# Further row tiles in seven products: third strips of the feed-forward parts, z's first and v's second block, the attention output's first block

## The chip, the cores and the metric

The kernel runs on one core of one Trainium2 chip. What counts is the device time of one execution, in microseconds. The time before is the median of three runs, 2545.25 us (2544.47 to 2546.2).

## What is computed

A trunk of two layers over x of 256 rows (T) and 2048 columns (D), all in float32, with weights that are read once per execution. The parts that matter here, of the reference:

```python
def swiglu(x, w_gate, w_up, w_down):
    return (jax.nn.silu(x @ w_gate) * (x @ w_up)) @ w_down

# layer 0: norm, one input projection, two mixers, one output projection
proj = (xn @ w_in).astype(f32)                    # q, k, v, o, gates, z, x, B, C, dt
...
y = y.reshape(b, s, SSD_D_INNER) * jax.nn.silu(z)
...
mixed = jnp.concatenate([hm, y], axis=-1).astype(xn.dtype)
return mixed @ w_out

# layer 1: norm, attention with 16 heads of 128
qkv = (xn @ w_qkv).astype(jnp.float32).reshape(b, s, 3, ATTN_HEADS, ATTN_HEAD_DIM)
...
o = o.transpose(0, 2, 1, 3).reshape(b, s, D_MODEL).astype(xn.dtype)
return o @ w_o
```

Each layer ends with x + swiglu(norm(x)), with 5632 hidden columns.

## The kernel before

**A product.** To keep float32 accuracy, each factor is split into a high and a low part in a shorter type, and each product is three matmuls: high by high, high by low, low by high. A weight tile `raw` (two row tiles of 128 by two strips of 512 columns, 512 KB) comes by a DMA that SyncE issues. ScalarE casts its high part, `wh` (L450); VectorE subtracts it and leaves the low part, `wl` (L452). `raw`, `wh` and `wl` live in buffers that rotate over three (`raw` has a fourth), so the cast for a tile waits until TensorE has done with the third tile before it.

**A block** (`block`) is one product of x with two strips of 512 columns: eight steps (six in a down projection with three strips), one for each pair of row tiles of the weights. A plan, a string of letters, gives the kind of each step; `pairs` says which row tile pairs the steps S take, in this order, and the steps P take the rest in ascending order.
- P, a plain step: 24 matmuls of 512 columns into four accumulators `acc_f` (F), which fill two double banks, `both`. Two casts, and two subtractions of 128x1024.
- S, a step in seven products (the scheme of Strassen and Winograd on two by two blocks: row tiles by columns): 21 matmuls, into F and into four more accumulators `acc_e` (E1, E7, E5, E6 in banks 4, 5, 6, 7). VectorE makes four sums of weights (L459 two of them, L460, L462), and then there are high and low parts of `raw` (three of its four pieces) and of `sums`. The factors on the other side are sums of x's blocks: `sums_of` and `activation_sums` (L331, L315 to L318), split again into high (ScalarE) and low (VectorE, L225), kept in a tile `skx` or `skh`.

After the last S of a block, E1 is copied to `pre` (L530), and E6, E7, E5 are added to it; after the last step F's accumulators are added (L1036 for z, L1067 in the feed-forward part, L961 in an output projection), which frees the banks.

**Order.** Each engine runs its instructions in a fixed order, which a scheduler makes from priorities: `high_priority` puts the parts of weights 800 places ahead, what empties `pre` 1600. Some pieces are put off (`later`, `transpose_later`) and run between steps: above all the transposes of y and of h, whose results `p_tr` sit in the same banks 6 and 7 as E5 and E6. Between the first and the last S of a block, none of them runs (`held`). Where a piece is needed sooner, `need` runs it.

**Places.** z is 2048 columns of the input projection in two blocks, q = 0 with `PLAN_LATE`, q = 1 with `PLAN_X`. While z's first block runs, the mLSTM output is turned (tiles `mx`, L226 on ScalarE, L227 on VectorE). The feed-forward part (`ffn`) takes the hidden columns in groups of 4, 4 and 3 strips of 512; each strip i is one block, `hidden`, of gate and up columns together, and after each group `add_blocks` multiplies the group's h with its rows of the down weights, in two blocks. The second strip (i = 1) of each group has `PLAN_X4` with four S steps, and makes the sums of pair 7 ahead of its fourth step; the other strips have `PLAN_X` with three. h's first block is summed as soon as it is turned, for the down projection (`skh`). v is made in two blocks (q = 0 `PLAN_LATE`, q = 1 `PLAN_X`). The attention output is added in two blocks, the first with `PLAN_O`, while the last heads (`attend_turn`: `p_pt`, copied to `pT`; `attend_out`: `p_o`, split into `o`) are still on their way.

## Time and profile before

| | |
|---|---|
| median of three runs | 2545.25 us (2544.47 to 2546.2) |
| the profiled execution | 2544.58 us |
| its span in the trace | 2542.8 us |
| granted TensorE clock | 0.999 |
| ScalarE, casts of weights and of their sums (L450) | 623.0 and 256.6 us busy |
| VectorE, low parts of weights and of their sums (L452) | 740.8 and 298.5 us busy |
| VectorE, sums of weights (L459, L460, L462) | 152.4, 85.7 and 85.7 us busy, 125 steps |

In the profile's rows PE is TensorE (matmuls), PEld its weight loads, DVE VectorE, ACT ScalarE, POOL GpSimd, SP SyncE. A row of a timeline has the start in us, the length, the engine, the line of the kernel, the operation, what it writes and reads, the shape, and how many in a row; in brackets the idle time ahead of it and what ended that. A row of the windows has, after the stretch, its length and for each engine the busy time with the number of instructions; then the granted clock, the share of DMA and GB/s. Lengths of one engine's instructions overlap a little in these rows, so that the price of one is the distance to the start of the next.

### The profile page before, as it was taken

To read this page: it belongs to the slowest core of one execution; us is meant where nothing else is said; L and a number is where in the kernel's file an instruction comes from. 1 tells how busy PE (TensorE), PEld (TensorE's weight loads), DVE (VectorE), ACT (ScalarE), POOL (GpSimd) and SP (SyncE) were. 2 spreads that over 40 slices of the span, in tenths; PEclk is the share of its full clock that TensorE was granted. 3 is DMA by queue.
4 is the path that set the end of the run, shared out by engine and by line. 5 is a ranking of instruction groups with operands and counts; after the bars stand their busy time and mean duration, and the time that the engine had idled before them with its cause. 6 is when DMAs were issued, how large, how long until landed. Compare 5 with 4: busy or idle time off the path is not lost.

```text
span 2542.8 us, 32518 instructions
## 1 busy us (share of the span) xinstructions
PE 2529.4 (99%) x12099; PEld 2118.3 (83%) x12099; DVE 2227.9 (88%) x2839; ACT 1483.9 (58%) x1968; POOL 48.5 (2%) x97
## 2 busy tenths in 40 slices
PE   9999999999999999999999999999999999999998
PEld 8888888888888888888888888888888888888887
DVE  5775788898989999999999986767999999999998
ACT  6465565566656655555455665666565555555564
POOL 1000000000000000000000000000000000000000
PEclk9999999999999999999999999999999999999999
DMA  8565575565565657565666656554556566656664
GB/s 289 174 214 180 170 227 171 177 209 188 191 218 178 224 175 231 192 222 187 218 206 208 198 175 231 165 167 146 199 191 208 200 204 215 214 198 197 227 200 166
DMA packets 256383, 505.40 MB, mean 199 GB/s; under 512 B 15976, under 2 KB 16128, under 8 KB 255712
## 3 DMA queue, kind: packets, MB, share of 16 engines
q1 hardware_dynamic: 249952, 483.20, 58.4%
q0 software_dynamic: 4976, 17.43, 1.8%
q10 hardware_dynamic: 1296, 2.69, 0.3%
q8 instruction: 95, 1.56, 0.2%
q14 instruction: 64, 0.52, 0.1%
HBM read 492.66 MB, written 2.14 MB: 195 GB/s over the span
## 4 chain that ended last, share of the span: by engine, by line
PE 95%; DVE 2%; DMA 1%; issue 1%; ACT 0%; POOL 0%; SPq 0%; POOLq 0%; DVEq 0%; ACTq 0%
PE acc_f L484 18%; PE acc_f L486 18%; PE acc_f L485 18%; PE acc_w L393 11%; PE acc_w L397 6%; PE acc_e L484 4%; PE acc_e L485 4%; PE acc_e L486 4%; PE acc_a L424 2%; PE acc_a L423 2%; PE acc_a L422 2%; PE p_tr L284 1%; DMA raw<-in_l_w_o 1%; PE p_y L919 1%; DVE wl L452 0%
## 5 line engine op out<-in xcount | busy, mean ns | idle before, releaser
L450 ACT CAST wh<-raw 128x1024 fp32r<-128x1024 f32 (+1 forms) x563 | 623.0, 1147 | 387.0 <-PE acc_f L486 313.8
L452 DVE TENSOR_TENSOR wl<-raw,wh 128x1024 fp32r<-128x1024 f32 (+1 forms) x563 | 740.8, 1338 | 84.8 <-ACT wh L450 81.4
L484 PE MATMUL acc_f<-wh,x 128*128 128x512 f32 x1086 | 424.8, 391 | 0.0
L486 PE MATMUL acc_f<-wh,x 128*128 128x512 f32 x1086 | 423.0, 389 | 0.0
L485 PE MATMUL acc_f<-wl,x 128*128 128x512 f32 x1086 | 422.7, 389 | 0.0
L450 ACT CAST wh<-sums 128x1024 fp32r<-128x1024 f32 x250 | 256.6, 1051 | 277.6 <-PE acc_f L486 135.0
L379 DVE TENSOR_TENSOR wl<-raw,wh 128x1024 fp32r<-128x1024 f32 x223 | 269.9, 1222 | 115.7 <-ACT wh L378 113.8
L378 ACT CAST wh<-raw 128x1024 fp32r<-128x1024 f32 x223 | 230.7, 1048 | 183.9 <-PE acc_w L393 94.7
L452 DVE TENSOR_TENSOR wl<-sums,wh 128x1024 fp32r<-128x1024 f32 x250 | 298.5, 1219 | 12.3 <-ACT wh L450 11.8
L393 PE MATMUL acc_w<-xa,wh 128*128 128x512 f32 x768 | 264.6, 395 | 1.2 <-DVE xa L227 1.2
L484 PEld LDWEIGHTS acc_f<-wh,x 128*128 128x128 f32 x1086 | 203.9, 188 | 43.0 <-DVE pre L1067 1.4
L486 PEld LDWEIGHTS acc_f<-wh,x 128*128 128x128 f32 x1086 | 203.9, 188 | 42.6
L485 PEld LDWEIGHTS acc_f<-wl,x 128*128 128x128 f32 x1086 | 203.9, 188 | 41.8
L397 PE MATMUL acc_w<-xa,wl 128*128 128x256 f32 x768 | 208.1, 281 | 0.5 <-DVE wl L379 0.5
L393 PE MATMUL acc_w<-x,wh 128*128 128x512 f32 x512 | 182.2, 399 | 0.0
L393 PEld LDWEIGHTS acc_w<-xa,wh 128*128 128x128 f32 x768 | 143.8, 188 | 31.7 <-ACT wh L371 1.5
L459 DVE TENSOR_TENSOR sums<-raw 128x1024 f32<-128x1024 f32 x125 | 152.4, 1219 | 7.0 <-DMA raw<-in_l_w_out 1.9
L397 PEld LDWEIGHTS acc_w<-xa,wl 128*128 128x128 f32 x768 | 142.0, 189 | 2.1 <-DVE wl L379 0.8
L397 PE MATMUL acc_w<-x,wl 128*128 128x256 f32 x512 | 143.3, 280 | 0.0
L393 PEld LDWEIGHTS acc_w<-x,wh 128*128 128x128 f32 x512 | 96.2, 188 | 20.5 <-DVE rsrc L430 0.4
L484 PE MATMUL acc_e<-wh,skx 128*128 128x512 f32 x261 | 101.7, 391 | 0.0
L486 PE MATMUL acc_e<-wh,skx 128*128 128x512 f32 x261 | 101.6, 389 | 0.0
(364 smaller groups left out, 4678.6 us busy)
## 6 DMA issues: line engine op xcount, KB each, us to landing
raw<-in_l_w_in SPq DMA_DIRECT2D x191, 512.0 KB, 3.8
raw<-in_l_ffn_gate SPq DMA_DIRECT2D x176, 512.0 KB, 4.0
raw<-in_l_ffn_up SPq DMA_DIRECT2D x176, 512.0 KB, 4.9
raw<-in_l_ffn_down SPq DMA_DIRECT2D x176, 512.0 KB, 5.1
raw<-in_l_w_qkv SPq DMA_DIRECT2D x96, 512.0 KB, 4.6
raw<-in_l_w_out SPq DMA_DIRECT2D x64, 512.0 KB, 4.9
raw<-in_l_w_o SPq DMA_DIRECT2D x32, 512.0 KB, 4.7
hr<-h POOLq DMA_DIRECT2D x32, 256.0 KB, 3.2
```

Source lines behind the costliest of these rows:

```text
L378: nc.scalar.copy(wh[:, ks, :], raw[:, ks, :])
L379: turn["low"] = nc.vector.tensor_sub(wl[:, ks, :], raw[:, ks, :], wh[:, ks, :].bitcast(F32))
L393: return nc.tensor.matmul(banks[f], wh[:, kk, f * P:(f + 1) * P], kt.both(k0 + kk), start=k0 + kk == 0, stop=False, skip_group_check=True)
L397: nc.tensor.matmul(banks[f][:, :T], wl[:, kk, f * P:(f + 1) * P], kt.parts(k0 + kk)[0], start=False, stop=k0 + kk == nk - 1, skip_group_ch ...
L422: nc.tensor.matmul(banks[t], xh[:, ts], wh[:, kk, :], start=k0 + kk == 0, stop=False)
L423: nc.tensor.matmul(banks[t], xh[:, ts], wl[:, kk, :], start=False, stop=False)
L450: nc.scalar.copy(h[:, c, :], of[:, c, :])
L452: nc.vector.tensor_sub(l[:, c, :], of[:, c, :], h[:, c, :].bitcast(F32))
L459: nc.vector.tensor_sub(sums[:, 0:2, :], raw[:, 2:4, :], raw[:, 3:0:-2, :])
L484: nc.tensor.matmul(dst, ah, bh, start=start, stop=False)
L485: nc.tensor.matmul(dst, ah, bl, start=False, stop=False)
L486: nc.tensor.matmul(dst, al, bh, start=False, stop=stop)
```

## The change

Nine plain steps become steps in seven products:
- z's first block: the plan "PPPSPSPP" becomes `PLAN_Z`, "PPPSPSSP", with the pairs 3, 5, 1 instead of 3 and 5: the new S comes right behind the second one, with the pair 1, whose sums were made in this block already for the one that follows; the plain steps are those of 0, 2, 4, 6, 7.
- the third strip (i = 2) of each of the six groups: `PLAN_X4` instead of `PLAN_X`. The sums of pair 7 are made in the second strip alone and used in the third too.
- v's second block: `PLAN_X4` instead of `PLAN_X`, with the sums of pair 7 made here.
- the attention output's first block: "PPPPPSPP" becomes "PPPPPSSP", with S for the pairs 1 and 3. The plain step of pair 6 then comes as the fifth, before both, and so do all heads of the last group.

```diff
--- before.py
+++ after.py
@@ -38,7 +38,8 @@
 PLAN_X = "PSPSPSPP"
 PLAN_X4 = "PSPSSPSP"
 PLAN_LATE = "PPPSPSPP"
-PLAN_O = "PPPPPSPP"
+PLAN_Z = "PPPSPSSP"
+PLAN_O = "PPPPPSSP"
 PLAN_SEAM = "PPPPSPSP"
 PLAN_H = {4: ("PSPSPSPP", "PSPSPSPP"), 3: ("PSPSPP", "PSPSPP")}
 PLAN_H_LATE = "PPSPSP"
@@ -1026,8 +1027,8 @@
             nc.scalar.activation(halves[i], halves[i], AF.Copy, scale=rr[:, i:i + 1])
 
     for q in range(2):
-        F, pre, _, _ = block(tuple((w_in, C_Z + (2 * q + n) * STRIP) for n in range(2)), xt0, 0, KD, PLAN_X if q else PLAN_LATE,
-                       ahead=((5, scale_gated, 0),) if q else ((4, sums_of, xt0, 1),))
+        F, pre, _, _ = block(tuple((w_in, C_Z + (2 * q + n) * STRIP) for n in range(2)), xt0, 0, KD, PLAN_X if q else PLAN_Z,
+                       pairs=(1, 3, 5) if q else (3, 5, 1), ahead=((5, scale_gated, 0),) if q else ((4, sums_of, xt0, 1),))
         if q == 0:
             for s in range(4):
                 need(("y", s))
@@ -1060,7 +1061,7 @@
         def hidden(hT, i, s, plan, copied):
             more = plan == PLAN_X4
             _, pre, both, joined = block(((wg_, s * STRIP), (wu_, s * STRIP)), xt, 0, KD, plan, pairs=(1, 3, 5, 7) if more else None,
-                                         ahead=((3, sums_of, xt, 7, False),) if more else ())
+                                         ahead=((3, sums_of, xt, 7, False),) if more and i == 1 else ())
             hs = []
             for t in range(NT):
                 with tc.high_priority(offset=1600):
@@ -1081,7 +1082,7 @@
             hT = KT(f"h{name}{first}", 4 * n)
             hT.sums = summed(PLAN_H[n][0])
             for i in range(n):
-                hidden(hT, i, first + i, PLAN_X4 if i == 1 else PLAN_X if first + i else PLAN_LATE, i < n - 1)
+                hidden(hT, i, first + i, PLAN_X4 if i in (1, 2) else PLAN_X if first + i else PLAN_LATE, i < n - 1)
             last = first + n == DFF // STRIP
             add_blocks(wd, hT, first * STRIP, 4 * n, (PLAN_H[n][0], PLAN_H_LATE if last and whole is None else PLAN_H[n][1]),
                        *((finish, begin, whole) if last else ()), pairs=list(hT.sums))
@@ -1169,7 +1170,8 @@
 
     vv = []
     for q in range(2):
-        F, pre, _, _ = block(tuple((w_qkv, 2 * D + (2 * q + n) * STRIP) for n in range(2)), xt2, 0, KD, PLAN_X if q else PLAN_LATE)
+        F, pre, _, _ = block(tuple((w_qkv, 2 * D + (2 * q + n) * STRIP) for n in range(2)), xt2, 0, KD, PLAN_X4 if q else PLAN_LATE,
+                             pairs=(1, 3, 5, 7) if q else None, ahead=((3, sums_of, xt2, 7),) if q else ())
         need("rope")
         for i in range(4):
             with tc.high_priority(offset=1600):
```

The scheduler places the instructions anew. No load is added, taken away or put in another place in SyncE's queue, nor is anything on GpSimd's. TensorE has 27 matmuls fewer, VectorE 42 instructions more, ScalarE 10. Line numbers of the changed kernel are one higher than those of before (two from v's block on), as the rows below show.

In z's first block, VectorE before, where the bank of the turned tile `p_tr_5069` is emptied (`mx3`), and the sums 5176 are those of the second S step:

```order
L227 SCALAR_TENSOR_TENSOR mx3_4897<-p_tr_5027,pv_129,mx3_4897 128x256
L462 TENSOR_TENSOR sums_5176<-raw_5173,sums_5176 128x512
L227 SCALAR_TENSOR_TENSOR mx3_4897<-p_tr_5069,pv_129,mx3_4897 128x256 x2
L452 TENSOR_TENSOR wl_5224<-raw_5220,wh_5223 128x1024
L452 TENSOR_TENSOR wl_5185<-sums_5176,wh_5184 128x1024 x2
L452 TENSOR_TENSOR wl_5224<-raw_5220,wh_5223 128x1024
```

And in the changed kernel, where 5214 are the sums of the third S step:

```order
L463 TENSOR_TENSOR sums_5176<-raw_5173,sums_5176 128x512
L461 TENSOR_TENSOR sums_5214<-raw_5211,sums_5214 128x512
L228 SCALAR_TENSOR_TENSOR mx3_4897<-p_tr_5027,pv_129,mx3_4897 128x256
L463 TENSOR_TENSOR sums_5214<-raw_5211,sums_5214 128x512
L453 TENSOR_TENSOR wl_5218<-raw_5211,wh_5217 128x1536
L228 SCALAR_TENSOR_TENSOR mx3_4897<-p_tr_5069,pv_129,mx3_4897 128x256
L453 TENSOR_TENSOR wl_5223<-sums_5214,wh_5222 128x1024 x2
L228 SCALAR_TENSOR_TENSOR mx3_4897<-p_tr_5069,pv_129,mx3_4897 128x256
L460 TENSOR_TENSOR sums_5345<-raw_5342 128x1024
L453 TENSOR_TENSOR wl_5185<-sums_5176,wh_5184 128x1024 x2
```

The second of the two `mx3` instructions on `p_tr_5069` now stands behind the low parts of the new step, `wl_5218` and `wl_5223`, and those of the second step, `wl_5185`, come after it.

ScalarE at the same place in the changed kernel, where `wh_5217` and `wh_5222` are the new step's high parts, and `pre_5249` the block's first result:

```order
L227 ACTIVATE mx3_4897<-p_tr_5069,pv_129 128x256
L451 CAST wh_5179<-raw_5173 128x1536
L451 CAST wh_5217<-raw_5211 128x1536
L451 CAST wh_5222<-sums_5214 128x1024 x2
L227 ACTIVATE mx3_4897<-p_tr_5069,pv_129 128x256
L531 COPY pre_5249<-acc_e_5111 128x512
L451 CAST wh_5184<-sums_5176 128x1024 x2
```

The last piece of `mx3` stands behind the casts of the new step; before it stood right behind `wh_5179`.

The second place is the end of the third strip in the group of three of the first feed-forward part, VectorE. Before, in the last S step of this strip (sums 11746), with `skh_11547`, the sums of h's first block:

```order
L452 TENSOR_TENSOR wl_11755<-sums_11746,wh_11754 128x1024
L462 TENSOR_TENSOR sums_11746<-raw_11743,sums_11746 128x512
L1071 SCALAR_TENSOR_TENSOR h_11557<-pre_11487,r1_7062,h_11557 128x512
L225 TENSOR_TENSOR skh_11547<-sf_11542,skh_11547 128x4x128
L452 TENSOR_TENSOR wl_11755<-sums_11746,wh_11754 128x1024
```

And in the changed kernel, where the sums 11958 and 12033 belong to the first and the second S step of the down projection that follows, and `skh_11562` are the sums of h's first block:

```order
L453 TENSOR_TENSOR wl_11967<-sums_11958,wh_11966 128x1024
L460 TENSOR_TENSOR sums_12033<-raw_12030 128x1024
L453 TENSOR_TENSOR wl_11967<-sums_11958,wh_11966 128x1024
L453 TENSOR_TENSOR wl_12001<-raw_11997,wh_12000 128x1024 x2
L461 TENSOR_TENSOR sums_12033<-raw_12030,sums_12033 128x512
L226 TENSOR_TENSOR skh_11562<-sf_11557,skh_11562 128x4x128
L463 TENSOR_TENSOR sums_12033<-raw_12030,sums_12033 128x512
```

`skh` was made inside the strip, and is now made behind the low parts of the down projection's first S step (`wl_11967`) and of the plain step after it (`wl_12001`).

## The prediction, made before the result was known

> **What bounds the kernel.** I read the page first: its shares of busy time, then the chain that ended last.

> ```profile
> span 2542.8 us, 32518 instructions
> PE 2529.4 (99%) x12099; PEld 2118.3 (83%) x12099; DVE 2227.9 (88%) x2839; ACT 1483.9 (58%) x1968; POOL 48.5 (2%) x97
> PE 95%; DVE 2%; DMA 1%; issue 1%; ACT 0%; POOL 0%; SPq 0%; POOLq 0%; DVEq 0%; ACTq 0%
> ```

> TensorE is on 95% of the chain: a matmul taken out is worth its time, unless the one behind it then waits. VectorE, at 88%, is what it would wait for. Next I read the timeline of PE for the price of a matmul.

> ```profile
> 1239.84 0.39 PE L484 MATMUL acc_f<-wh,ha 128*128 128x512 f32 x1
> ...
> 1241.65 0.39 PE L486 MATMUL acc_f<-wh,ha 128*128 128x512 f32 x1
> ```

> These are the first and the last of nine matmuls, eight starts apart: 1.81/8 = 0.227 us each. The 0.39 us is a length that overlaps the next one's; the pitch is what counts.

> Then the price of a step on VectorE, from its timeline in the third strip of a three-strip group. Starts are again what counts.

> ```profile
> 1368.13 2.35 DVE L452 TENSOR_TENSOR wl<-raw,wh 128x1024 fp32r<-128x1024 f32 x2
> 1370.40 1.22 DVE L459 TENSOR_TENSOR sums<-raw 128x1024 f32<-128x1024 f32 x1
> 1371.53 1.75 DVE L452 TENSOR_TENSOR wl<-raw,wh 128x1536 fp32r<-128x1536 f32 x1
> 1373.20 0.69 DVE L460 TENSOR_TENSOR sums<-raw,sums 128x512 f32<-128x512 f32 x1
> 1373.80 1.22 DVE L452 TENSOR_TENSOR wl<-sums,wh 128x1024 fp32r<-128x1024 f32 x1
> 1374.94 0.69 DVE L462 TENSOR_TENSOR sums<-raw,sums 128x512 f32<-128x512 f32 x1
> 1376.21 0.69 DVE L225 TENSOR_TENSOR skh<-sf,skh 128x512 fp32r<-128x512 f32 x1
> ```

> A plain step costs 2.27 us there (1368.13 to 1370.40). A step of seven products costs 1.13 + 1.67 + 0.60 + 1.14 + 0.60 and one more 1.14 (the second sums piece): 6.28 us, so 4.0 us more. Last, how much room VectorE has, by stretches: here the six blocks of a four-strip group, of which the first stretch is about a third strip, then the third strip of a three-strip group, and v's second block.

> ```profile
> 840.00:882.00 42.00, 42.00 (x190) 34.55 (x190) 41.55 (x46) 25.11 (x27) 1.08 (x2) 1.00 0.65 216
> 882.00:924.00 42.00, 42.00 (x191) 34.82 (x191) 38.96 (x43) 24.29 (x26) 1.08 (x2) 1.00 0.64 214
> ...
> sum 255.00, PE 255.00 PEld 210.64 DVE 239.89 ACT 142.76 POOL 3.23; mean PE 42.50 PEld 35.11 DVE 39.98 ACT 23.79 POOL 0.54
> 1351.00:1392.30 41.30, 41.30 (x187) 34.12 (x187) 40.84 (x44) 25.25 (x29) 1.07 (x2) 1.00 0.69 229
> 1490.00:1531.50 41.50, 41.50 (x186) 34.35 (x186) 36.38 (x40) 23.57 (x26) 0.00 (x0) 1.00 0.59 195
> ```

> The third column of busy time is VectorE's. Over a whole group 255.0 − 239.9 = 15 us are free, but in a third strip only 0.45 us of 42 (0.46 of 41.3 in the group of three), and 3.0 in the fourth strip (the second row). v's second block has 5.1 us free.

> **The change, part by part.**

> *The gain.* Nine steps go from 24 to 21 matmuls: 27 × 0.227 = 6.1 us, 0.68 us each. This much is sure as far as PE's instruction count goes; all else is what PE then waits for. [...]

> *z's first block (one step): +3.2 us net.* Two steps of seven products now stand side by side, and a PSUM bank that a transposed tile (p_tr_5069) still holds is freed too late. Rows of before, VectorE, ScalarE and PE:

> ```profile
> 527.53 0.48 DVE L227 SCALAR_TENSOR_TENSOR mx<-p_tr,pv,mx 128x256 fp32r<-128x256 f32 x1
> 528.55 0.48 DVE L227 SCALAR_TENSOR_TENSOR mx<-p_tr,pv,mx 128x256 fp32r<-128x256 f32 x1 [0.55 <-ACT mx L226]
> 530.82 1.23 DVE L452 TENSOR_TENSOR wl<-raw,wh 128x1024 fp32r<-128x1024 f32 x1 [1.79 <-ACT wh L450]
> 528.04 0.48 ACT L226 ACTIVATE mx<-p_tr,pv 128x256 fp32r<-128x256 f32 x1 [4.17 <-DVE mx L227]
> 530.70 1.99 ACT L450 CAST wh<-sums 128x1024 fp32r<-128x1024 f32 x2
> 531.99 0.39 PE L486 MATMUL acc_e<-wh,xa 128*128 128x512 f32 x1
> ```

> In before both mx pieces on VectorE are done at 529.0, two of them in a row, with 1.79 us idle after them. In the changed order the second one stands behind wl_5223 x2, the low parts of the new step's sums, and ScalarE's piece behind the casts wh_5222 x2. Those casts need a buffer of the three that rotate: wh_5143's went to wh_5217, so it is wh_5179's, whose last reader is the PE row above, at 531.99; three matmuls of the bank (acc_e_5123) now come behind it, so 531.99 − 0.68 = 531.31, ended at 531.7. Two casts take 1.99: 533.7. VectorE's second subtraction follows, 1.2: 534.9, then mx, 0.48: the bank is free at about 535.5. PE gets to acc_e_5123 ten matmuls after 531.31, at 533.6, and 0.3 later for wl_5218, made just too late: 533.9. **It waits 1.6.** Only then are the last readers of wh_5099 done (three matmuls, 0.7: 536.2), whose buffer wh_5184's casts need: 1.0 for the first, 1.0 for the second, and wl_5185 1.2 behind. PE has four matmuls ready, and waits 1.3 + 0.5. With 0.2 for the later start of z's second block: 0.3 + 1.6 + 1.8 + 0.2 = 3.9, less 0.68: 3.2. Bounds: −0.7 (all hidden, if the casts find a buffer earlier) and +4.5 (0.6 more at the seam to the second block, the size of a 512-wide piece). I take 3.2, nearest to the rows.

> *Third strips of four-strip groups (four steps): −0.1 each.* Nothing in before shows a third strip with four such steps, but its second strips already have four, and two more sums of x. There PE is late only where the next strip begins. Rows of before at such a seam:

> ```profile
> 846.42 1.05 ACT L450 CAST wh<-sums 128x1024 fp32r<-128x1024 f32 x1 [4.00 <-PE acc_f L486]
> 846.81 0.46 PE L484 MATMUL acc_e<-wh,x 128*128 128x512 f32 x1
> 847.18 0.50 PE L484 MATMUL acc_f<-wh,x 128*128 128x512 f32 x1
> ```

> The cast waits for the buffer of the last plain step; PE starts 0.37 apart where 0.23 is usual (0.14), and some 0.1 more at the next. The changed third strip gets this seam too: 0.25. VectorE enters the next strip 4.0 later, with 3 us free there, and pre's evacuation (L1067) holds a bank that the strip's second half needs: about 0.3 more, a bound from the 0.68 of one such 512 piece. 0.6 − 0.68 = −0.1 each, −0.4 in all. The four sums of pair 7 that are not made again cost nothing: they are kept from the second strip. Ends: −0.4 each (seam alone) and +2 (below).

> *Third strips of three-strip groups (two): +1.8 each.* After them comes the down projection, whose second step needs the sums of the first h block (skh). In before it was ready at 1376.21, inside the strip. Now the low part's instruction stands behind the first step's wl, the next plain step's wl x2 and a sum. Rows of before:

> ```profile
> 1394.57 2.35 DVE L452 TENSOR_TENSOR wl<-sums,wh 128x1024 fp32r<-128x1024 f32 x2
> 1396.84 1.22 DVE L459 TENSOR_TENSOR sums<-raw 128x1024 f32<-128x1024 f32 x1
> 1399.35 0.39 PE L484 MATMUL acc_f<-wh,skh 128*128 128x512 f32 x1
> ```

> VectorE is done with those wl at 1396.84 in before; now + 4.0 for the new step, + 1.13 (L459 of the next one, moved ahead), − 1.2 (skh and one ha piece, moved behind), − 0.46 (what was idle): 1400.3. Then wl x2 2.27, a sum 0.60, skh 0.69: **1403.9**. PE's first matmul with skh was at 1399.35; now 0.68 earlier, two matmuls moved ahead (0.45) and 0.3 at the seam: 1399.4. That one and the second read only the high part, which ScalarE makes; the one that reads the low part comes ten later: 1401.7. It waits 2.2, from which I take 0.2 for idle that I count double. With the seam's 0.3 and 0.2 for the bank behind it: 2.5 − 0.68 = 1.8. Twice: +3.6. Ends: −0.4 (VectorE 2 us earlier than I add up) and +3 each.

> *v's second block (one): −0.7.* VectorE idles in the block, waiting for ScalarE (the first three rows); the last two are pieces of a sum of x, as another block makes it:

> ```profile
> 1510.73 2.36 DVE L452 TENSOR_TENSOR wl<-raw,wh 128x1024 fp32r<-128x1024 f32 x2 [1.97 <-ACT wh L450]
> 1519.36 1.23 DVE L452 TENSOR_TENSOR wl<-sums,wh 128x1024 fp32r<-128x1024 f32 x1 [1.12 <-ACT wh L450]
> 1531.14 3.71 DVE L452 TENSOR_TENSOR wl<-raw,wh 128x1024 fp32r<-128x1024 f32 x3 [0.98 <-ACT wh L450]
> ...
> 1766.59 0.67 DVE L331 TENSOR_TENSOR xg<-o 128x512 f32<-128x512 f32 x1
> 1767.30 0.29 DVE L315 TENSOR_TENSOR sf<-xg 128x128 f32<-128x128 f32 x1
> ```

> These, and the 5.1 us of the stretch, take the 4.0 of the step; the extra sums of x (two pieces of 512, 0.6 from start to start, and four of 128, 0.2 each: 2.0) take the rest, 6.0 against 5.1 and the lead that VectorE has. Ends −0.7 and +0.6, if the rest falls on the seam.

> *Attention output's first block (one): +0.5.* The plain step of pair 6 goes two steps ahead, and with it the last two heads' p_o, whose pT copies stand behind the new order's two sums casts:

> ```profile
> 1769.01 1.99 ACT L450 CAST wh<-sums 128x1024 fp32r<-128x1024 f32 x2 [0.41 <-PE acc_f L486]
> 1771.43 0.85 ACT L1159 COPY pT<-p_pt 128x384 f32<-128x384 f32 x2
> 1770.56 0.38 PE L1166 MATMUL p_o<-pT,v 128*128 128x128 f32 x2
> ```

> In before PE had another plain step between the p_o of heads 0 and 1 (done at 1770.9) and those of 2 and 3. Now the latter follow at once. Casts done at 1770.9, the copies 0.4 each: 1771.3 and 1771.7; PE, ready at 1770.9, waits 0.4 for the first, and up to 0.4 more for the second and the casts of o. 0.7, and 0.5 for a later evacuation at the second block's start, less 0.68: +0.5. Ends −0.7 and +1.5. SP's queue gets no other order of loads and no more of them, and POOL's stays as it is: nothing there.

> *The sum.* 3.2 − 0.4 + 3.6 − 0.7 + 0.5 = +6.2. The profiled execution took 2544.58 us (span 2542.8), 0.67 under the median of 2545.25. 2544.58 + 6.2 = 2550.8; set against the median, 2551.4. I predict 2551.

> **Rivals.** The bound for a difference is 0.2%, 5.1 us either way.

> A. *VectorE's lead hides it all*: −6.1, 2538.4 to 2539. For it: 15 us free in each group, 1.79 idle in z just where the new sums stand. It needs the low part of skh by 1401.7 (2.2 us sooner than I add up) and z's bank by 533.6 (1.9 sooner): both orders speak against it. [...] In v's block the rows bear it out, at the seams they don't.

> B. *One of the two large stalls isn't there*: without z's 3.9, +2.3 (2546.9); without the two 2.2 at the down projection, +1.8 (2546.4). Both large stalls rest on a chain of four or five steps with some 0.3 us error each, and one earlier release is enough. Within 0.2%.

> C. *VectorE's deficit stays inside the third strips*: 40.85 or so busy and 4.0 more against 40.6 us of PE: 4 us late, and if its lead in front of PE is only 2 us, PE waits 2 us in each of the four: 2544.6 + 6.2 + 8.4 = 2559. Against it stand the second strips of before, with as many sums and no wait inside.

> **How the numbers follow.** Forecast 0.48, A 0.09, B 0.33, C 0.10. Of the forecast, 0.05 lies below 2550.3. Faster 0.09; same 0.33 + 0.05 = 0.38; slower 0.43 + 0.10 = 0.53. The range, 2543 to 2556, takes in B and the forecast with z at its +4.5 and the three-strip groups at their +3, and leaves out A and C.

> **What would show it.** 27 fewer matmuls on PE. In z's first block a gap of PE of over 1 us ahead of acc_e, released by VectorE's mx (L228 now), and a second behind it, released by ScalarE's cast of sums. At the start of the down projections of both three-strip groups a wait of about 2 us for VectorE's skh; none over 0.4 us in the four-strip groups; none in v. Wrong it would be if skh's low part comes before the plain step's wl, or the mx before wl_5223 has waited, or if the gaps sit in the third strips themselves.

## The result

The changed kernel took 2566.78 us, the median of five runs (2562.74 to 2570.81), against 2544.85 us before: a ratio of 1.0085, 95% interval 1.0071 to 1.0099. It is slower, the side that was forecast, but by 21.9 us and not by 6, and outside the range. The profiled execution is the longest of the five, 2570.81 us, so its parts below add up to 26 us and not to 22. First the page of the changed kernel, the same lines as of before.

```profile
span 2569.0 us, 32521 instructions
PE 2541.0 (99%) x12072; PEld 2117.7 (82%) x12072; DVE 2264.4 (88%) x2881; ACT 1497.2 (58%) x1978; POOL 49.1 (2%) x97
PE 86%; DVE 8%; issue 3%; DMA 2%; ACT 1%; SPq 0%; POOL 0%; POOLq 0%; DVEq 0%; ACTq 0%
```

The 27 matmuls are gone (12099 to 12072), as the change says. The chain shows the price: TensorE fell from 95% to 86% of it, VectorE rose from 2% to 8%. The busy share of PE, 99% in both, shows nothing of it.

Where the time went, read from the same instruction in both traces (the adding of the F accumulators at a block's end, L961, L1036 and L1067 of before):

| end of | before, us | changed, us | later by |
|---|---|---|---|
| the first output product (z's blocks and all ahead) | 629.38 | 637.11 | 7.7 |
| first layer, first group of four | 972.27 | 981.25 | 9.0 |
| second group of four | 1224.18 | 1233.66 | 9.5 |
| group of three, second down block | 1457.66 | 1469.74 | 12.1 |
| v's second block | 1545.65 | 1558.71 | 13.1 |
| attention output, second block | 1834.77 | 1852.48 | 17.7 |
| second layer, groups of four | 2299.97 | 2319.39 | 19.4 |
| the last block (here an adding of `pre`) | 2531.09 | 2557.11 | 26.0 |

Not all of this was lost at changed places. At 500 us, ahead of all of them, the changed kernel's trace is already 0.8 us late, and the other traces lie between −1.4 and +1.5 us there. So z's blocks cost 7.0 of the 7.7 us.

Now the waits of TensorE in the changed kernel, from its timeline (in brackets the idle time and what ended it):

```profile
536.54 0.47 PE L485 MATMUL acc_e<-wh,skx 128*128 128x512 f32 x1 [1.53 <-DVE mx L228]
538.61 0.74 PE L485 MATMUL acc_e<-wh,skx 128*128 128x512 f32 x2 [1.13 <-ACT wh L451]
540.85 0.79 PE L486 MATMUL acc_e<-wl,skx 128*128 128x512 f32 x1 [0.56 <-DVE wl L453]
598.12 0.50 PE L485 MATMUL acc_f<-wh,mx 128*128 128x512 f32 x1 [0.73 <-DVE pre L1037]
956.51 0.50 PE L485 MATMUL acc_e<-wh,skh 128*128 128x512 f32 x1 [0.78 <-DVE ha L226]
1413.63 0.50 PE L487 MATMUL acc_f<-wh,skh 128*128 128x512 f32 x1 [1.80 <-DVE skh L226]
...
1785.21 0.70 PE L1166 MATMUL p_o<-pT,v 128*128 128x256 f32 x2 [0.49 <-ACT pT L1160]
1808.18 0.50 PE L485 MATMUL acc_f<-wh,o 128*128 128x512 f32 x1 [0.76 <-DVE xres L962]
1847.82 1.09 PE L285 MATMUL p_tr<-ident_r,xres 128*128 128x128 f32 x8 [1.67 <-DVE pre L545]
2512.29 0.50 PE L485 MATMUL acc_f<-wh,hb 128*128 128x512 f32 x1 [1.69 <-ACT wh L451]
```

The first three and the one at 1413.63 are the waits that the prediction named, near the sizes that it gave. The wait of 0.78 at 956.51 goes against it: "none over 0.4 us in the four-strip groups". And behind the long ones there is something that it did not have. Rows of the timeline and of the windows (after the busy times the granted clock, the share of DMA and GB/s):

```profile
1415.43 0.63 PE L485 MATMUL acc_f<-wh,ha 128*128 128x512 f32 x1
1415.86 0.63 PE L486 MATMUL acc_f<-wl,ha 128*128 128x512 f32 x1
1416.29 0.63 PE L487 MATMUL acc_f<-wh,ha 128*128 128x512 f32 x1
...
2499.00:2504.00 5.00, 4.45 (x12) 3.53 (x13) 4.80 (x7) 2.71 (x3) 0.00 (x0) 0.66 0.87 311
2504.00:2512.00 8.00, 6.61 (x33) 5.08 (x31) 5.81 (x10) 5.21 (x7) 0.00 (x0) 1.00 0.61 206
2512.00:2517.00 5.00, 4.69 (x12) 3.51 (x13) 2.18 (x3) 1.64 (x3) 0.00 (x0) 0.66 0.66 211
```

The starts stand 0.43 us apart in place of 0.227: the clock is halved (granted 0.50 from 1414.37 to 1417.78). A mean of 0.66 over 5 us is 3.4 us at half clock, and then it is 1.00 again. Added up over the trace, between neighbouring matmuls of `block`: distances of 0.43 us cost 5.6 us in excess of 0.227 (0.4 before), the other distances over 0.28 us cost 28.8 (7.9 before). With the 6.1 us gained that is 20 of the 26 us. The rest lies outside `block`: some 3.5 us at transposes (the row of 1847), 1.6 in the product behind v's blocks, and the 0.8 at the start.

### The profile page after: what moved, and what is told of

It is laid out like the page before. It is cut to its first block, busy times and chain, and to the rows that moved or that the text cites. A ratio compares the mean times of both kernels' runs of the same rounds, so it can differ in the third digit from the quotient of the medians.

```text
span 2569.0 us, 32521 instructions
## 1 busy us (share of the span) xinstructions
PE 2541.0 (99%) x12072; PEld 2117.7 (82%) x12072; DVE 2264.4 (88%) x2881; ACT 1497.2 (58%) x1978; POOL 49.1 (2%) x97
## 4 chain that ended last, share of the span: by engine, by line
PE 86%; DVE 8%; issue 3%; DMA 2%; ACT 1%; SPq 0%; POOL 0%; POOLq 0%; DVEq 0%; ACTq 0%
PE acc_f L485 16%; PE acc_f L487 16%; PE acc_f L486 16%; PE acc_w L394 11%; PE acc_w L398 6%; PE acc_e L486 4%; PE acc_e L487 4%; PE acc_e L485 4%; DVE wl L453 4%; PE acc_a L425 2%; PE acc_a L424 2%; PE acc_a L423 2%; ACT wh L451 1%; DMA raw<-in_l_ffn_down 1%; DVE sums L460 1%
## 5 line engine op out<-in xcount | busy, mean ns | idle before, releaser
L451 ACT CAST wh<-sums 128x1024 fp32r<-128x1024 f32 x268 | 276.1, 1051 | 331.4 <-PE acc_f L487 143.6
L485 PE MATMUL acc_f<-wh,x 128*128 128x512 f32 x1044 | 408.3, 391 | 0.4
L487 PE MATMUL acc_f<-wh,x 128*128 128x512 f32 x1044 | 406.7, 390 | 0.0
L486 PE MATMUL acc_f<-wl,x 128*128 128x512 f32 x1044 | 406.3, 389 | 0.0
L453 DVE TENSOR_TENSOR wl<-sums,wh 128x1024 fp32r<-128x1024 f32 x268 | 320.6, 1219 | 6.3 <-ACT wh L451 5.2
L485 PEld LDWEIGHTS acc_f<-wh,x 128*128 128x128 f32 x1044 | 195.9, 188 | 42.9 <-DVE pre L1068 3.0
L487 PEld LDWEIGHTS acc_f<-wh,x 128*128 128x128 f32 x1044 | 196.0, 188 | 41.0
L486 PEld LDWEIGHTS acc_f<-wl,x 128*128 128x128 f32 x1044 | 196.0, 188 | 40.1
L460 DVE TENSOR_TENSOR sums<-raw 128x1024 f32<-128x1024 f32 x134 | 163.2, 1218 | 12.3 <-DMA raw<-in_l_ffn_down 4.0
L485 PE MATMUL acc_e<-wh,skx 128*128 128x512 f32 x270 | 104.8, 394 | 3.3 <-ACT wh L451 1.7
L486 PE MATMUL acc_e<-wl,skx 128*128 128x512 f32 x270 | 106.0, 394 | 0.9 <-DVE wl L453 0.9
```

What stands on the lines that cost most here:

```text
L451: nc.scalar.copy(h[:, c, :], of[:, c, :])
L453: nc.vector.tensor_sub(l[:, c, :], of[:, c, :], h[:, c, :].bitcast(F32))
L460: nc.vector.tensor_sub(sums[:, 0:2, :], raw[:, 2:4, :], raw[:, 3:0:-2, :])
L485: nc.tensor.matmul(dst, ah, bh, start=start, stop=False)
L486: nc.tensor.matmul(dst, ah, bl, start=False, stop=False)
L487: nc.tensor.matmul(dst, al, bh, start=False, stop=stop)
```

## The experiments

Every ratio is against before, measured beside it on the same chip; "of before" and "of changed" say which kernel was edited.

**One place alone.** Of before, each with one part of the change.

```diff
z_alone
-xt0, 0, KD, PLAN_X if q else PLAN_LATE,
+xt0, 0, KD, PLAN_X if q else PLAN_Z, pairs=(1, 3, 5) if q else (3, 5, 1),
four_alone, three_alone (each with ahead=... if more and i == 1)
-PLAN_X4 if i == 1 else PLAN_X if first + i else PLAN_LATE
+PLAN_X4 if i == 1 or i == 2 and n == 4 else PLAN_X if first + i else PLAN_LATE
+PLAN_X4 if i == 1 or i == 2 and n == 3 else PLAN_X if first + i else PLAN_LATE
o_alone
-PLAN_O = "PPPPPSPP"
+PLAN_O = "PPPPPSSP"
v_alone
-xt2, 0, KD, PLAN_X if q else PLAN_LATE)
+xt2, 0, KD, PLAN_X4 if q else PLAN_LATE,
+pairs=(1, 3, 5, 7) if q else None, ahead=((3, sums_of, xt2, 7),) if q else ())
```

> Before with the change in z's first block alone. Theory P (the costs belong to places, and each is the waits that the changed kernel's trace shows there, with a stretch of half clock behind the longest): +7.7 us, of which some 5.5 us of waits in z's first block, 1.2 us of half clock behind them and 1.0 us at the end of z's second block, less 0.7. Rival Q (the sum of the prediction was right place by place, and the rest is VectorE's lateness carried from one changed place into the next, which needs all of them together): +3.2 us, and no wait at the end of z's second block.

> Before with PLAN_X4 in the third strips of the four-strip groups alone (4 steps). Theory P: +3.4 us in all, about 0.6 us of waits at each third-to-fourth seam and 0.2 to 1.2 us at each down projection, nothing of half clock. Rival Q: -0.4 us, and no wait at the down projections.

> Before with PLAN_X4 in the third strips of the three-strip groups alone (2 steps). Theory P: +9.9 us (+3.3 in the first layer, +6.6 in the second), with a wait of 1.8 to 2 us for skh in each and the granted clock under 0.9 in the 5 us behind each. Rival Q: +3.6 us, the same two waits and no second wait in the second layer; clock as in before.

> Before with the new plan of the attention output's first block alone. Theory P: +4.7 us, of which 1.0 us at the start of its second block, 0.7 us in it, 0.5 us at p_o and 1.9 us at the transposes behind it. Rival Q: +0.5 us.

> Before with v's second block alone. Theory P (costs as in the changed kernel's trace at the place): +0.2 us. Rival Q (the prediction's term: VectorE's idle time takes it): -0.7 us. Either is within the noise of a measurement, and the trace tells: P has a wait of 0.5 us or more at the start of the next product, Q none.

| | median | before | change | ratio, 95% interval |
|---|---|---|---|---|
| z_alone | 2552.13 | 2544.65 | +7.5 | 1.0018 to 1.0038 |
| four_alone | 2557.22 | 2544.65 | +12.6 | 1.0041 to 1.0066 |
| three_alone | 2554.51 | 2544.65 | +9.9 | 1.0027 to 1.0054 |
| o_alone | 2547.07 | 2544.65 | +2.4 | 1.0000 to 1.0018 |
| v_alone | 2545.29 | 2544.57 | +0.7 | 0.9993 to 1.0011 |

z and the groups of three cost alone about what they cost in the whole: theory P. So their excess over the prediction (3.2 and 3.6) isn't lateness carried from place to place. Not all of z_alone's +7.5 is z's: its trace, of a shorter execution (2550.27), loses 5.1 us in z's blocks and 1.7 in the attention output, which the edit doesn't touch. The attention output costs half of P's 4.7. v's time can't be told from none. The surprise is four_alone, which costs nearly four times what its places do in the changed kernel, and the five add up to 33 us where the whole costs 22. Its trace loses 3.4 us up to the end of the second group of four, twice what P has for these two groups, then 6.9 us between 1835 and 1879 (times of before), where the edit touches nothing, and 6.9 us more in the second layer's groups, four times what P has there. Hence the next run.

**Order far away.** Of before, two of the four steps of four_alone, those of the first layer:

```diff
-PLAN_X4 if i == 1 or i == 2 and n == 4 else PLAN_X if first + i else PLAN_LATE
+PLAN_X4 if i == 1 or i == 2 and n == 4 and name == "a" else PLAN_X if first + i else PLAN_LATE
```

> Before with PLAN_X4 in the third strips of the two four-strip groups of the first layer alone. Theory T (a changed plan moves the scheduler's order in parts that the change doesn't touch: in the four-strip run's order four transposes of xres stand some 20 matmuls earlier in the attention output's second block than in before, and there that run's PE waited 3.5 us for them): +1.7 us at the changed strips, and the wait of some 3.5 us with half clock again in the second layer, 350 us after the last changed strip; +7 to +9 us. Rival U (time and load carried along, not order): +1.7 us, and nothing there.

It took 2554.62 against 2544.57: +10.1, ratio 1.0025 to 1.0051. Its timeline in the attention output's second block, some 660 us behind the last changed strip, and then the row of before at the first of these transposes that waits:

```profile
1843.51 0.66 PE L284 MATMUL p_tr<-ident_r,xres 128*128 128x128 f32 x2 [3.47 <-DVE xres L961]
1844.82 0.69 PE L284 MATMUL p_tr<-ident_r,xres 128*128 128x128 f32 x2 [0.66 <-DVE xres L961]
```

```profile
1842.58 0.98 PE L284 MATMUL p_tr<-ident_r,xres 128*128 128x128 f32 x7 [0.24 <-DVE xres L961]
```

In before these transposes waited 0.24. In before's order 48 matmuls stand between these transposes and those of the strips ahead of them, in this kernel's 24, and so they come before VectorE has their input (4 and then 12, where before has 8 and 8); the lag grows from 2.9 us at 1834.8 to 10.0 at 1879 (times of before). Theory T: a plan that is changed in one layer moves the scheduler's choices in another, and such a move can cost more than the change. The strips themselves cost 3.7 us here, where the same two steps cost 1.7 in the changed kernel. In the changed kernel the same place has yet another order, and loses some 3 us (1847.82 above).

**Only priority?** VectorE has some idle time around z's stall, and the scheduler puts work of low priority last in its order; if that is all, placing the starved work ahead cures it. Of the changed kernel, in three steps, and the three steps on before:

```diff
h_ahead, then m_ahead, in transpose_split
-with tc.high_priority(offset=1200 if first else 0):
+with tc.high_priority(offset=1200 if first or kt.name[0] == "h" else 0):
+with tc.high_priority(offset=1200 if first or kt.name[0] in "hm" else 0):
mh_ahead, and b_all_ahead on before: that of m_ahead, and in hidden
+with tc.high_priority(offset=1400):
     nc.scalar.activation(h, g, AF.Silu, scale=r[:, t:t + 1])
     nc.vector.scalar_tensor_tensor(h, u, r[:, t:t + 1], h, op0=OP.mult, op1=OP.mult)
```

> The changed kernel, with the emptying of turned h tiles and their sums placed 1200 ahead in the scheduler's order, so that skh's low part stands inside the third strip again. Theory R (VectorE has time enough over some 10 us, but in a full stretch it takes work of low priority last, and PE waits for just that): the two waits for skh, 1.8 us each, and the half clock behind them go, 8 to 9 us less than the changed kernel, 2558. Rival S (VectorE is simply overfull at this seam): the wait moves to the weights' low parts behind it, and the time stays within 2 us of the changed kernel's 2566.8.

> As h_ahead, and the emptying of the turned mLSTM tiles (mx) placed 1200 ahead too. Theory R: z's first wait (1.5 us, for mx), the wait for the casts behind it (1.1 us) and 1.2 us of half clock go; 4 to 6 us less than h_ahead. Rival S: the sums' low parts come later by as much, and the wait stays under another name; within 2 us of h_ahead.

> As m_ahead, and silu and product of h (L1071, L1072 of the changed kernel) placed 1400 ahead too, in the changed kernel. In m_ahead the wait for skh had gone and PE waited 3.9 us for h itself, the next work of low priority at the same seam (6.7 to 7.2 us there with the half clock behind it, in each layer). Theory R (VectorE has the time, it is the order in which a full stretch serves its work): both waits go, about 13 us less than m_ahead, near 2551. Rival S (overfull): the wait moves on to a third instruction at the seam, the weights' low parts; within 3 us of m_ahead's 2564.5.

> The kernel before with the same three changes of priority and no step changed: what they do by themselves. Theory R: nothing in before is starved, so within 1.5 us of before. Rival: the priorities alone bring several us, and then the gain of the mended kernels isn't the cure of the change's waits.

| | median | before | ratio, 95% interval |
|---|---|---|---|
| changed | 2566.78 | 2544.85 | 1.0071 to 1.0099 |
| h_ahead | 2568.01 | 2544.57 | 1.0076 to 1.0102 |
| m_ahead | 2564.46 | 2544.57 | 1.0062 to 1.0090 |
| mh_ahead | 2572.17 | 2545.24 | 1.0090 to 1.0118 |
| b_all_ahead | 2549.10 | 2545.24 | 1.0006 to 1.0024 |

For z, theory R holds: in m_ahead none of the three waits of z's first block is left, and the lag at 629.38 is 0.3 us in place of 7.7. Less what each trace was late at 500 us, z's blocks then cost nothing, and 0.5 us with the same priorities without the change (b_all_ahead), so the step brings 0.6 of its 0.7. But the priorities by themselves cost before 3.9 us, more than the 1.5 that theory R allowed. For the three-strip groups neither R nor S holds as stated. h_ahead freed skh, and PE waited for the next thing; mh_ahead freed that too, and then the weights' low parts came late, in the strip itself and in the four-strip groups as well. One row each of m_ahead, then of mh_ahead:

```profile
1416.86 1.54 PE L285 MATMUL p_tr<-ident_r,h 128*128 128x128 f32 x6 [3.88 <-DVE h L1072]
```

```profile
900.40 0.50 PE L486 MATMUL acc_e<-wl,skx 128*128 128x512 f32 x1 [0.84 <-DVE wl L453]
1395.12 0.50 PE L486 MATMUL acc_e<-wl,skh 128*128 128x512 f32 x1 [0.94 <-DVE wl L453]
```

Three names in turn, and the bill stays: mh_ahead took no less than the changed kernel, part of which is what the priorities cost by themselves.

**The amount and the place of the work.** What is left is the amount of work (4.0 us more in a strip with 0.5 free), or where it falls: PLAN_X4 has its last S step at step 6 and not at step 5 (counted from 0), so that adding up E (2.3 us) falls on the seam. Both apart and together, on three_alone, and for all groups on the changed kernel. "Light" leaves out the low parts of two steps' sums in the changed strips, with the high part in their place, 4.5 us of VectorE's work per strip; TensorE and ScalarE do the same work.

```diff
light, in weights, for the pairs 3 and 5 of the changed strips
+h = high_unit(4)
+for c in (slice(0, 2), slice(2, 4)):
+    nc.scalar.copy(h[:, c, :], sums[:, c, :])
+return first + (h, h)
-return first + parts(sums, (slice(0, 2), slice(2, 4)))
early, in the changed strips
-PLAN_X4 = "PSPSSPSP"
+PLAN_X6 = "PSPSSSPP"
```

three_light, three_early and three_light_early are three_alone with the one, the other and both; all_light and all_early are the changed kernel with the one or the other in all six groups.

> three_alone with less work for VectorE: in the two changed strips the low parts of the weights' sums are left out in two of the four steps in seven products (the high part stands in for them), 4 subtractions of 128x1024 or 4.5 us per strip; TensorE and ScalarE do as much as before. Theory S (capacity: the 4.0 us that the new step adds to a strip in which VectorE has 0.5 us free have to be paid by PE, whatever the order): the 9.9 us go, less 1.4 for the matmuls and with 0.25 at each seam and about 1 us that moved elsewhere: +0.5 us against before, 2545, no wait for skh and no second wait. Rival V (it is ScalarE's casts and the three rotating buffers that a fourth step in seven products holds up): the waits stay, +6 us or more.

> The changed kernel with the same left out in the third strips of all six groups (pairs 3 and 5). Theory S: what the third strips cost goes (13.3 us in the changed kernel's trace, its own gain of 4.1 already counted in), and they gain: 2566.8 - 13.3 - 4.1 + 1.5 for the seams, near 2551; z's 7.7 us and the attention output's 4.7 us stay, with the half clock behind z's wait. Rival V: 2563 or more.

> three_alone with the plan PSPSSSPP in place of PSPSSPSP: the same four steps in seven products, the last of them one step earlier, as in before, so that VectorE adds E1, E6, E7, E5 up (2.3 us) under two plain steps and not at the seam. Theory W (it is the lump of work that the later last step throws on the seam): the two seams fall to 0.5 us each or less, and the time to before or 1 us over it; three steps side by side may cost up to 1 us inside the strip. Theory S (the amount of work in the strip): +9.9 us stays within 2.

> three_early with the low parts of two sums left out as in three_light (the high part stands in for them), 4.5 us less for VectorE per strip. Theory W and S together (both must go for the seam to be free): 0 to -1.5 us against before, apart from the 1 to 2 us that three_alone and three_light lose at the attention output's second block, where their order differs from before. W alone: as three_early. S alone: +9 us as three_light.

> The changed kernel with PSPSSSPP in the third strips of all groups. Theory W: 2566.8 less the 9.9 us of the three-strip groups and their gain of 1.4, less 2 to 3 us at the seams of the four-strip groups: 2553, z's and the attention output's waits staying. Theory S: within 3 us of 2566.8.

| against before, us | last S at step 6 | last S at step 5 |
|---|---|---|
| full work | three_alone +9.9 (1.0027 to 1.0054) | three_early +19.4 (1.0061 to 1.0089) |
| light | three_light +9.2 (1.0022 to 1.0050) | three_light_early −0.6 (0.9989 to 1.0007) |

Only both together free the seam. three_light_early has no wait at either seam (below first its windows there, where the PE column is full, and then the first seam of three_light), and keeps the gain: its trace is 1.2 us ahead of before at 1391 (times of before), of which 0.6 from ahead of the strip and 0.65 in it, the price of three matmuls. The second strip gains as much, and the attention output's second block, which the edit doesn't touch, takes 1.3 us back. three_light has 3.9 us free in the strip, and still waits at the seam:

```profile
1388.00:1412.00 24.00, 24.00 (x110) 19.24 (x109) 22.83 (x29) 14.03 (x18) 0.00 (x0) 1.00 0.55 175
2463.00:2487.00 24.00, 24.00 (x113) 19.63 (x113) 22.87 (x29) 13.91 (x17) 0.00 (x0) 1.00 0.64 213
...
1389.00:1413.00 24.00, 21.58 (x93) 16.56 (x92) 22.27 (x27) 9.57 (x12) 0.00 (x0) 0.93 0.63 208
...
1353.00:1395.00 42.00, 41.90 (x189) 34.12 (x187) 38.12 (x42) 25.63 (x28) 1.07 (x2) 1.00 0.61 204
...
1406.69 0.50 PE L490 MATMUL acc_e<-wl,ha 128*128 128x512 f32 x1 [1.51 <-DVE wl L452]
1407.90 0.50 PE L491 MATMUL acc_f<-wh,ha 128*128 128x512 f32 x1 [0.70 <-DVE ha L225]
```

three_early with full work is far worse: with three S steps side by side VectorE is so late that the copy and the sums of E come late, and PE waits for the banks that they free:

```profile
1394.74 0.50 PE L485 MATMUL acc_e<-wh,ha 128*128 128x512 f32 x1 [1.67 <-ACT pre L531]
1396.11 0.77 PE L283 MATMUL p_tr<-ident_r,hr 128*128 128x128 f32 x4 [0.40 <-DVE pre L532]
1397.93 0.77 PE L485 MATMUL acc_e<-wh,skh 128*128 128x512 f32 x1 [1.05 <-DVE pre L533]
1400.20 0.72 PE L283 MATMUL p_tr<-ident_r,hr 128*128 128x128 f32 x4 [1.07 <-DVE pre L536]
1401.93 0.76 PE L485 MATMUL acc_f<-wh,ha 128*128 128x512 f32 x1 [1.01 <-DVE pre L1068]
```

all_light took 2561.63 (1.0053 to 1.0079), 5 us less than the changed kernel, where theory S had 16: the four-strip groups cost next to nothing then (the lag goes from 4.4 us ahead of them to 4.1 at their ends in the first layer), the three-strip seams still cost, as in three_light. all_early took 2601.9 us, the median of four executions (1.0207 to 1.0235), 35 over the changed kernel, where theory W had 14 less; a fifth execution took 14609.82 us, and why is open. So theory W alone and theory S alone both fall: at the three-strip seams each remedy alone leaves the other cause. Rival V (ScalarE's casts and the rotating buffers) had the time of three_light, +6 us or more; but the waits at its seam above are for VectorE, and three_light_early makes the same casts without a wait. Two things stay open. Light and early together were not run in all six groups, so that the cure is shown for the three-strip groups alone. And every one of these edits also gives a new order to all parts, so that some of each difference may be theory T's.

## Why the prediction was wrong

Its mechanisms were found where it put them, and its sign was right; the sum was 6.2 and is 22 (26 in the profiled execution). Two of its readings are a little off, and move the sum by 0.2 at most: the pieces of 512 in v stand 0.71 us apart in the row shown, not 0.6, and the casts of the attention output are done at 1771.0, not 1770.9.

- *The gain*: 27 matmuls fewer at 0.227, 6.1 us. Right.
- *z, +3.2*: the mechanism was right and its waits fit: 1.53 for mx (1.6 in the text), 1.13 and 0.2 for the casts (1.3), 0.56 for wl_5185 (0.5). By start distances the waits are 5.7 us and not 3.9, as the matmul behind each wait starts some 0.1 us late too (536.54 to 536.85: 0.31 in place of 0.227). Missing are 1.2 us of half clock, and 1.0 us at the end of z's second block (598.12), where the lateness comes out again. Measured +7.0 in the changed kernel's trace, +7.5 as the whole of z_alone.
- *Four-strip groups, −0.4*: the seam was right (0.8 us more than before by start distances, 0.6 in the text). Missing are the down projections behind them, 0.1 to 0.9 us more than before each (956.51 above): the text asked what is late in the next strip, and not what the strip's h is late for. +3.4 in the changed kernel's trace, and more where the order is another (four_alone, four_first).
- *Three-strip groups, +3.6*: the wait for skh is 1.80 in the first layer and as long in the second (2.0 in the text). Missing are the half clock behind it, and in the second layer one more wait of 1.69, where ScalarE's cast of a sum comes behind it. three_alone: +9.9.
- *v, −0.7*: right within the block. The first matmul behind v's blocks, in the timeline of before and then of v_alone, starts 0.71 us earlier, with no wait ahead of it:

```profile
1545.45 0.40 PE L393 MATMUL acc_w<-x,wh 128*128 128x512 f32 x1
```

```profile
1544.74 0.40 PE L393 MATMUL acc_w<-x,wh 128*128 128x512 f32 x1
```

  That the whole of v_alone is not faster (+0.7, −1.8 to +2.8) lies behind it: in the 50 us that follow, in a product that the edit doesn't touch, the matmuls stand a little further apart without a wait, and the lag goes from −0.7 to +0.9 us. The changed kernel loses the same 1.6 us there. Why is open.
- *Attention output, +0.5*: p_o's wait came as said (0.49), and the start of the second block waits 0.76 (0.5 in the text). o_alone: +2.4. In the whole, 2 us more by the order of the transposes of xres behind it.

The failed step, in its own words, is "all else is what PE then waits for": each wait was looked for at one place, and priced at its length. The sum has 12.3 us of lost time (6.2 and the 6.1 gained), the trace 32. Of the 20 us between them, what the runs showed is this. Four of the five waits of TensorE of 1.5 us or more in this trace (1.53 in z with 1.13 behind it, 1.80, 1.79 and 1.69, but not 1.67 at the transposes) were followed by 3.41 us at a granted clock of 0.50. That cost 5.2 us in all (the 5.6 above less the 0.4 of before), and there is no term for it. The late starts in `block` come to 20.9 us in place of 12.3, above all because lateness is paid again at the next places where VectorE's or ScalarE's work gates a matmul (598.12, 956.51, 2512.29). And "nothing there" was said of the untouched parts from SP's and POOL's queues alone, while VectorE's and TensorE's orders there had moved: some 5 us more stand outside `block`, at transposes and in the product behind v's blocks. Rival C (a deficit of VectorE paid in the four-strip groups, +8) had the right cause and mostly the wrong place: the four-strip groups cost 3.4 us, and the three-strip groups, where no slack strip follows, 10.8 in this trace.

The pitch stayed as the sum has it outside the slow stretches (17 distances from 1848.98 to 1852.86, 0.228 us each). On the clock the changed kernel's trace shows half rate behind 1.80 us of idle time (1413.63), for 3.41 us (0.50 from 1414.37 to 1417.78).

## What to carry over

An engine that was 99% busy in a stretch (VectorE, 40.84 of 41.30 us) could not take 4 us more there, whatever the average over the kernel says. Moving priorities only renamed the wait there; it cured the one in z, where the engine had idle time. Ask for each added step which stretch has both the room and a seam that doesn't depend on it. Price a wait of the tensor engine of over 1.5 us with a chance of the slow clock behind it (here four times of five, 3.41 us at 0.50 each). And where a scheduler sets the order, compare the order of every part, not only the changed ones: four_first lost more in an untouched part than in its own.

## What the runs showed of the hardware

```profile
1403.03 0.50 PE L486 MATMUL acc_f<-wh,skh 128*128 128x512 f32 x1 [1.79 <-DVE skh L225]
...
2482.09 0.50 PE L486 MATMUL acc_f<-wh,skh 128*128 128x512 f32 x1 [1.78 <-DVE skh L225]
...
1401.49:1404.90 3.41, 1.87 (x7) 1.25 (x8) 3.41 (x7) 1.34 (x1) 0.00 (x0) 1.00 0.99 344
1404.90:1408.31 3.41, 3.41 (x17) 2.53 (x16) 3.31 (x6) 1.38 (x3) 0.00 (x0) 1.00 0.63 223
2480.11:2483.52 3.41, 1.61 (x6) 0.90 (x6) 3.41 (x6) 0.90 (x1) 0.00 (x0) 1.00 0.97 339
2483.52:2486.93 3.41, 3.41 (x9) 2.63 (x9) 3.32 (x5) 1.82 (x3) 0.00 (x0) 0.50 0.67 252
```

The last of these windows is a slow stretch of this trace; the other edges are laid back from its start, 2483.52, in multiples of 3.413 us. So laid, the second wait lies whole within one window, which has 1.80 us without a matmul (3.41 less 1.61); the first is cut by the edge at 1401.49, and its window has 1.54.

The multiple is that of the changed kernel's trace. Its stretches at 0.50 ahead of the kernel's end begin at 540.56, 1414.37, 2499.81 and 2513.46, the later ones 256, 574 and 578 times 3.413 us behind the first, and each lasts 3.413 us. Laid out from them, six windows of this trace have more than 1 us of idle time between matmuls. Here they are in order of time, the first value behind the length being PE's busy time:

```profile
533.73:537.14 3.41, 1.88 (x9) 1.21 (x7) 2.67 (x3) 1.79 (x3) 0.00 (x0) 1.00 0.80 263
537.14:540.55 3.41, 1.81 (x6) 0.59 (x4) 2.12 (x2) 1.99 (x2) 0.00 (x0) 1.00 0.12 46
1410.96:1414.37 3.41, 1.61 (x7) 1.02 (x6) 3.41 (x6) 0.20 (x1) 0.00 (x0) 1.00 0.90 281
1844.45:1847.86 3.41, 1.71 (x12) 1.11 (x10) 3.41 (x6) 2.96 (x5) 0.00 (x0) 1.00 0.82 281
2496.40:2499.81 3.41, 1.62 (x8) 1.04 (x7) 3.41 (x5) 0.46 (x1) 0.00 (x0) 1.00 0.82 247
2510.05:2513.46 3.41, 1.71 (x7) 0.85 (x6) 3.41 (x4) 2.71 (x4) 0.00 (x0) 1.00 0.39 129
```

Behind four of them, with 1.60, 1.80, 1.79 and 1.70 us idle, stands a window at 0.50. Behind the other two, with 1.53 us at 533.73 and 1.70 at the transposes (1844.45), the clock stays at 1.00. That the idle time within such a window counts, and not the length of a wait, is an estimate from these six windows and the two of three_alone. But for the one at the transposes it fits all of them: 1.53 and 1.54 us without, 1.60 to 1.80 with half clock behind. No run moved a wait across an edge to test it. It fits, too, that the runs of the changed kernel scatter over 8 us (2562.74 to 2570.81, granted clock 0.998 to 0.996 in this order), and those of before, with no half clock but at the kernel's end (0.50 from 2537.38), over 1.7.
